# Hybrid decoder trunk, one core: the conditioning sum of the expert stage in its first blocks, the second mixer's sums in its attention, and another pace of the gathers

## The chip, the cores and the metric

The kernel runs on one core of one Trainium2 chip. The metric is the time of one execution on the device, in microseconds (us), as the median of several runs. The numbers of the profile come from one profiled execution of the same program. MB and GB are powers of ten.

## What is computed

A trunk of two residual layers over 512 positions of width 1024. Each layer is a token mixer and then a feed-forward part that retrieves experts by product keys. Before both, the input is normalized and modulated by shift, scale and gate vectors that come from a condition `c`:

```python
c_act = jax.nn.silu(c)
for layer in range(DEPTH):
    mod = (c_act @ ada_w[layer] + ada_b[layer])[:, None, :]
    sh1, sc1, g1, sh2, sc2, g2 = jnp.split(mod, 6, axis=-1)
    h = rmsnorm(x, norm_mix[layer]) * (1.0 + sc1) + sh1
    y = even_mixer(h, ...) if layer % 2 == 0 else odd_mixer(h, ...)
    x = x + g1 * y
    h = rmsnorm(x, norm_ffn[layer]) * (1.0 + sc2) + sh2
    x = x + g2 * peer_ffn(h, peer_w_q[layer], peer_sub_keys[layer], peer_u[layer], peer_v[layer])
return rmsnorm(x, norm_final)
```

`c_act @ ada_w` is a product of one row with a matrix of 1024 x 6144 per layer. The program calls each sixth of it (1024 x 1024, the pieces m = 0 to 5) a conditioning sum. Every position picks 128 experts (8 heads, 16 each) of 16384; an expert is one row of U and one of V:

```python
act = jax.nn.gelu(jnp.einsum('cd,ced->ce', xc, u[ec]))
return jnp.einsum('ce,ced->cd', gc.astype(xc.dtype) * act, v[ec])
```

## The kernel before, in words

**Whole program.** Four stages follow one another: the even mixer (layer 0), the expert stage of layer 0, the odd mixer (layer 1), the expert stage of layer 1. Each float32 product is made from three products of split operands (high and low part, `mm3`, lines 146 to 150): ScalarE makes the high part (line 162), VectorE the low part (line 163). The program is written as one sequence; a scheduler then sets the order on each engine, and each engine and each DMA queue works its list in that order. `issue_after` pins instructions behind a given one.

**The expert stage** (`peer`). Positions come in four blocks of 128. For the first three (384 positions) all 16384 experts are computed densely, in 128 blocks of 128 experts, and weighted by a gate matrix that is zero where an expert was not picked. For the last 128 positions the picked rows of U and V are gathered.

- Dense part: block i needs its U tile (512 KB; `u_block`, 24 matmuls of 384 columns, tile `ups`), then gelu (tile `gl`), the product with the gates (tile `wf`, line 1445), its split (`weh`, `wel`), its V tile (512 KB) and 18 matmuls of 512 columns that add to six PSUM banks `y`. Gate values come by DMA for eight blocks at a time (tile `gt`, 1.5 MB, line 1442). U and V tiles are loaded on the SP queue into tiles called `raw`, three buffers in all, which the whole program shares; the split tiles `wh`, `wl` have three buffers too. Already during routing 51 U blocks are computed ahead, so the main loop makes a U block and a V product in blocks 0 to 76 and a V product alone in blocks 77 to 124; three more V products follow at the end. These last 51 blocks are called the last stretch here.
- Gathered part (`gather_steps`): step k gathers 128 rows of U (tile `gu`, 128x1024, GpSimd's queue, line 1551), VectorE multiplies and sums them (line 1558); from step 16 on it also gathers the V rows of 16 steps before (`gv`), and VectorE adds them to the accumulator `acc` (128x1024 in SBUF, line 1566). From step 128 on only `gv` is left. How many steps are due at block i is set by two numbers: GU per block in blocks 0 to 76, GV per block after. `acc` is set to zero at the beginning of the stage (line 1427).
- Conditioning sum of the next layer (`ada_late`, first stage only): for each half of 512 columns, four loads of 512 KB (two pieces of the weights, tile `araw`, also in a `raw` buffer, line 259), two VectorE operations per load (lines 263 and 265) that add in a PSUM bank, a copy by ScalarE into another `raw` buffer (`asum`, line 268), and four small matmuls that sum over the partitions (line 271). It is put in from block 76 on, a quarter of a step per block (EP = 0.25).

**The odd mixer** (`odd`). Projections of V in two halves, then 64 attention units (8 head pairs, 2 heads, 4 position blocks) in a loop of 67 passes (`run_units`), with the remaining projections as filler. The four conditioning sums m = 2, 4, 3, 5 of layer 1 (`ada`, line 238 load of 256 KB in a `raw` buffer, lines 240 and 242 on VectorE) run as background, `self.bg`, 64 steps in all: `step(n % 2)` takes 12 of them in the second half of the V projection, and the attention loop takes OB = 0.75 per pass. What is left is done at the end.

## Time and profile before

| | |
|---|---|
| median of 3 runs | 3201.61 us (3197.92 to 3205.02) |
| profiled execution | 3189.73 us, span of its instructions 3187.9 us |
| mean granted TensorE clock | 0.992 |
| even mixer, layer 0 | about 0 to 350 us |
| expert stage, layer 0 | main loop from 746 us, last stretch 1394 to 1625 us |
| odd mixer, layer 1 | about 1625 to 1940 us |
| expert stage, layer 1 | main loop from 2321 us, last stretch 2969 to 3179 us |

PE is TensorE, PEld its weight loads, DVE VectorE, ACT ScalarE, POOL GpSimd, SP the engine whose queue issues most loads; a "q" behind the name means the queue. A window's row gives, for each engine, the busy time in us and the number of instructions, then the granted TensorE clock (1.00 is 2.4 GHz), the mean busy share of the 16 DMA engines and the rate. A wait's row gives who waited for whom, the sum, the number and the longest. A timeline's row ends with the idle time of the engine before it and what ended it.

### The profile page before, as it was taken

The numbers are of one execution on the slowest core, as the hardware profiler recorded it, in microseconds if no ns is written. First come the engines' busy times: TensorE is split into PE (matmuls) and PEld (weight loads), VectorE is DVE, ScalarE is ACT, GpSimd is POOL, SyncE is SP. The second block draws the span as 40 slices with busy tenths as digits, with TensorE's granted clock in tenths as the row PEclk, the third lists the DMA queues.
The fourth block names the chain that finished last, engine by engine and source line by source line (L and its number), as shares of the span: only waits on it lengthen the run. The fifth ranks groups of instructions, "written<-read, shape, count | busy, mean of one in ns | idle before, by whom it ended". The sixth has DMA issues, their size and how long they took to land.

```text
span 3187.9 us, 45266 instructions
## 1 busy us (share of the span) xinstructions
PE 3089.2 (97%) x16416; PEld 2681.4 (84%) x16416; DVE 2593.8 (81%) x5112; ACT 1371.3 (43%) x2294; POOL 711.3 (22%) x564
## 2 busy tenths in 40 slices
PE   8999999999999999998999999999999999999998
PEld 5766788998998898987777878899989998899887
DVE  6988799996777777887766888999867887788887
ACT  5566524553333333333355764245533333333333
POOL 0000000002444444432210000000024444444331
PEclk9999999999999999999999999999999999999999
DMA  7325323658899899997733333245588998899885
GB/s 244 133 86 175 108 90 124 229 223 290 290 319 331 320 336 325 334 320 282 264 129 129 127 109 112 93 171 224 216 289 317 324 338 325 314 328 336 310 318 191
DMA packets 304064, 758.91 MB, mean 238 GB/s; under 512 B 24328, under 2 KB 125248, under 8 KB 297696
## 3 DMA queue, kind: packets, MB, share of 16 engines
q1 hardware_dynamic: 225120, 480.04, 42.8%
q0 software_dynamic: 74240, 268.54, 23.2%
q10 hardware_dynamic: 4480, 7.44, 0.7%
q8 instruction: 128, 2.10, 0.3%
q14 instruction: 96, 0.79, 0.1%
HBM read 698.96 MB, written 56.64 MB: 237 GB/s over the span
## 4 chain that ended last, share of the span: by engine, by line
PE 60%; DMA 17%; DVE 16%; issue 4%; ACT 3%; POOL 0%; SPq 0%; DVEq 0%; ACTq 0%; POOLq 0%
DMA gv<-in_peer_v_dram,eidx 9%; PE ups L150 7%; PE y L149 7%; PE y L148 7%; PE y L150 7%; PE ups L148 7%; PE ups L149 7%; DVE wl L163 3%; PE pp L149 3%; PE pp L148 3%; PE pp L150 3%; DMA araw<-in_ada_w_dram 2%; DMA raw<-in_peer_v_dram 2%; DMA gu<-in_peer_u_dram,eidx 2%; PE gps L1312 1%
## 5 line engine op out<-in xcount | busy, mean ns | idle before, releaser
L162 ACT ACTIVATE wh<-raw 128x1024 fp32r<-128x1024 f32 x602 | 635.6, 1056 | 1015.6 <-PE ups L149 472.2
L163 DVE TENSOR_TENSOR wl<-raw,wh 128x1024 fp32r<-128x1024 f32 x602 | 734.2, 1220 | 111.3 <-ACT wh L162 110.2
L148 PE MATMUL ups<-h2h,wh 128*128 128x384 f32 x2048 | 693.0, 338 | 9.4 <-ACT h2h L162 4.8
L150 PE MATMUL ups<-h2h,wl 128*128 128x384 f32 x2048 | 693.7, 339 | 7.3 <-DVE wl L163 7.2
L149 PE MATMUL ups<-h2l,wh 128*128 128x384 f32 x2048 | 689.5, 337 | 0.7 <-DVE h2l L163 0.7
L1551 POOL DMA_INDIRECT gu<-in_peer_u_dram,eidx x256 | 290.4, 1134 | 1608.0 <-DVE eidx L1410 1165.1
L148 PE MATMUL y<-wh,weh 128*128 128x512 f32 x1536 | 602.3, 392 | 19.8 <-ACT wh L162 10.7
L149 PE MATMUL y<-wl,weh 128*128 128x512 f32 x1536 | 603.9, 393 | 3.1 <-DVE wl L163 3.1
L150 PE MATMUL y<-wh,wel 128*128 128x512 f32 x1536 | 602.7, 393 | 0.0
L1551 POOL DMA_INDIRECT gv<-in_peer_v_dram,eidx x256 | 395.9, 1546 | 555.2 <-DVE gu L1558 360.6
L1566 DVE SCALAR_TENSOR_TENSOR acc<-gv,act,acc 128x1024 f32<-128x1024 f32 x256 | 328.3, 1282 | 152.4 <-DMA gv<-in_peer_v_dram,eidx 151.5
L148 PEld LDWEIGHTS ups<-h2h,wh 128*128 128x128 f32 x2048 | 385.7, 188 | 17.9 <-ACT h2h L162 5.3
L150 PEld LDWEIGHTS ups<-h2h,wl 128*128 128x128 f32 x2048 | 385.2, 188 | 12.5 <-DVE wl L163 12.4
L149 PEld LDWEIGHTS ups<-h2l,wh 128*128 128x128 f32 x2048 | 385.6, 188 | 7.7 <-DVE h2l L163 1.2
L1558 DVE SCALAR_TENSOR_TENSOR gu<-gu,htm 128x1024 f32<-128x1024 f32 x256 | 312.3, 1220 | 60.5 <-DMA gu<-in_peer_u_dram,eidx 60.2
L148 PEld LDWEIGHTS y<-wh,weh 128*128 128x128 f32 x1536 | 290.1, 189 | 79.7 <-ACT wh L162 12.4
L149 PEld LDWEIGHTS y<-wl,weh 128*128 128x128 f32 x1536 | 289.9, 189 | 63.9 <-DVE wl L163 6.3
L150 PEld LDWEIGHTS y<-wh,wel 128*128 128x128 f32 x1536 | 289.7, 189 | 60.9 <-DVE wel L163 0.2
L162 ACT ACTIVATE weh<-wf 128x384 fp32r<-128x384 f32 x256 | 133.5, 524 | 480.8 <-PE y L149 356.0
L163 DVE TENSOR_TENSOR wel<-wf,weh 128x384 fp32r<-128x384 f32 x256 | 141.6, 554 | 81.3 <-ACT weh L162 80.5
L1445 DVE TENSOR_TENSOR wf<-gl,gt 128x384 f32<-128x384 f32 x256 | 140.0, 553 | 11.5 <-DMA gt<-gates 10.7
L1189 ACT ACTIVATE gl<-ups 128x384 f32<-128x384 f32 x256 | 121.4, 474 | 0.1
(411 smaller groups left out, 4252.2 us busy)
## 6 DMA issues: line engine op xcount, KB each, us to landing
raw<-in_peer_uT_dram SPq DMA_DIRECT2D x256, 512.0 KB, 4.5
raw<-in_peer_v_dram SPq DMA_DIRECT2D x256, 512.0 KB, 4.3
gates<-gst SPq DMA_DIRECT2D x48, 1024.0 KB, 5.0
gt<-gates SPq DMA_DIRECT2D x32, 1536.0 KB, 12.4
araw<-in_ada_w_dram SPq DMA_DIRECT2D x176, 256.0 KB, 3.1
raw<-in_peer_wq_dram SPq DMA_DIRECT2D x32, 512.0 KB, 3.3
raw<-in_odd_w_dram SPq DMA_DIRECT2D x25, 512.0 KB, 3.3
raw<-in_even_w_dram SPq DMA_DIRECT2D x23, 512.0 KB, 3.4
```

The lines of the kernel that those rows point to most:

```text
L148: mm(out, a[0], b[0], start=start, stop=False)
L149: mm(out, a[0], b[1], start=False, stop=False)
L150: mm(out, a[1], b[0], start=False, stop=stop)
L162: self.lact = nc.scalar.activation(hi, src, AF.Copy)
L163: self.last = nc.vector.tensor_tensor(lo, src, hi.bitcast(F32), op=ALU.subtract)
L1189: nc.scalar.activation(gl, ps[:, :ND], AF.Gelu_apprx_tanh)
L1312: nc.tensor.matmul(ps[:, z], oh[:, t, 1], og[:, t, 0], start=True, stop=False)
L1445: nc.vector.tensor_tensor(wf.rearrange("p (c t) -> p c t", t=CT), gls[i].rearrange("p (c t) -> p c t", t=CT), self.gt[:, :, i % IG], op=AL ...
L1551: nc.gpsimd.indirect_dma_start(out=r, out_offset=None, in_=table, in_offset=bass.IndirectOffsetOnAxis(ap=eidx[:, k:k + 1], axis=0))
L1558: nc.vector.scalar_tensor_tensor(r, r, 1.0, htm, op0=ALU.mult, op1=ALU.mult, accum_out=act[:, k:k + 1])
L1566: nc.vector.scalar_tensor_tensor(acc, r, act[:, j:j + 1], acc, op0=ALU.mult, op1=ALU.add)
```

## The change

Four things are done.

1. The conditioning sum of the first expert stage (`ada_in` in place of `ada_late`) is put in from block 0 on, one step per block, and adds in the two halves of `acc` in SBUF. The copy by ScalarE and its `raw` buffer are gone; the small matmuls read `acc`.
2. `acc` is set to zero just ahead of gather step 16, the first that adds to it, in both expert stages.
3. GU goes from 1.44 to 1.40, GV from 0.62 to 0.70, in both expert stages.
4. In the odd mixer the sums start behind the V projection, and the attention loop takes one step per pass.

```diff
-GU = 1.44
-GV = 0.62
+GU = 1.4
+GV = 0.7
+GRP = 16
-EP = 0.25
-OB = 0.75
+OB = 1
...
-    def ada_late(self, layer, m, psum, tag):
+    def ada_in(self, layer, m, sums, psum, tag):
...
-            acc = self.bank(psum, tag)
+            acc = sums[:, s]
...
                 yield 1
-            sb = self.stream.tile([P, D], F32, tag="raw", name=self.nm("asum"))[:, :T]
-            nc.scalar.activation(sb, acc, AF.Copy)
             ps = self.bank(psum, tag)
             for b in range(4):
-                nc.tensor.matmul(ps[:, b:b + 1], sb[:, b * P:(b + 1) * P], self.ones[:, 0:1], start=True, stop=True)
+                nc.tensor.matmul(ps[:, b:b + 1], acc[:, b * P:(b + 1) * P], self.ones[:, 0:1], start=True, stop=True)
...
-            self.bg = [self.ada(layer, m, ah, psum, "tr", 0) for m in (2, 4, 3, 5)]
-            for n, _ in enumerate(more):
-                self.step(n % 2)
+            for _ in more:
+                pass
...
             fl.add("out", self.out_early(layer, I["odd_wo"], 0, psum, lambda: done))
+            self.bg = [self.ada(layer, m, ah, psum, "tr", 0) for m in (2, 4, 3, 5)]
...
         acc = fin.tile([P, D], F32, name=self.nm("acc"))
-        nc.vector.memset(acc, 0.0)
...
-        self.bg = [self.ada_late(l, m, self.pu, "u") for l, m in ([] if last else [(layer + 1, 0)])]
-        steps = 0.0
+
+        self.bg = [] if last else [self.ada_in(layer + 1, 0, acc, self.pu, "u")]
...
                 while ng < due:
+                    if ng == GRP:
+                        self.step(1000)
+                        nc.vector.memset(acc, 0.0)
                     ng += 1
                     next(gather, None)
-                if i >= NK - AHEAD:
-                    steps += EP
-                    self.step(int(steps))
-                    steps -= int(steps)
+                self.step(1)
```

How the order of the instructions moves is shown at three places. A row is line, operation, output, inputs and shape; the number behind a name tells the buffers apart.

SP at the start of the first expert stage, before (`gates` is the gate matrix on its way to memory, `in_peer_uT` and `in_peer_v` are U and V):

```order
L170 DMA raw_7999<-in_peer_v_dram 128x1024
L1317 DMA gates_3612<-gst_7714 128x2048
L170 DMA raw_8035<-in_peer_uT_dram 128x1024
L170 DMA raw_8068<-in_peer_v_dram 128x1024
L1442 DMA gt_7997<-gates_3612 128x24x128
L170 DMA raw_8101<-in_peer_uT_dram 128x1024
L1442 DMA gt_8539<-gates_3612 128x24x128
L170 DMA raw_8134<-in_peer_v_dram 128x1024
L170 DMA raw_8170<-in_peer_uT_dram 128x1024
L170 DMA raw_8203<-in_peer_v_dram 128x1024
```

and in the change:

```order
L170 DMA raw_7998<-in_peer_v_dram 128x1024
L1315 DMA gates_3612<-gst_7714 128x2048
L259 DMA araw_8034<-in_ada_w_dram 128x2x512
L1439 DMA gt_7996<-gates_3612 128x24x128
L170 DMA raw_8038<-in_peer_uT_dram 128x1024
L170 DMA raw_8071<-in_peer_v_dram 128x1024
L1439 DMA gt_8576<-gates_3612 128x24x128
L259 DMA araw_8104<-in_ada_w_dram 128x2x512
L170 DMA raw_8108<-in_peer_uT_dram 128x1024
L170 DMA raw_8141<-in_peer_v_dram 128x1024
```

The first gate tile stands ahead of the next U and V tile and behind the first load of the sum; from then on each U and V pair has a load of the sum ahead of it, eight in all.

VectorE at the same place, from the last step of routing, before:

```order
L1269 TENSOR_TENSOR r_7901<-m_1636_7895 128x128
L1427 MEMSET acc_7958 128x1024
L163 TENSOR_TENSOR wl_7906<-raw_7903,wh_7905 128x1024
L1410 TENSOR_TENSOR eidx_3322<-ef,r_7901 128x128
L163 TENSOR_TENSOR wl_8002<-raw_7999,wh_8001 128x1024
L163 TENSOR_TENSOR wl_8038<-raw_8035,wh_8037 128x1024
L1445 TENSOR_TENSOR wf_8005<-gl_3645,gt_7997 128x384
L1445 TENSOR_TENSOR wf_8074<-gl_3714,gt_7997 128x384
L163 TENSOR_TENSOR wel_8008<-wf_8005,weh_8007 128x384
```

and in the change:

```order
L1267 TENSOR_TENSOR r_7901<-m_1636_7895 128x128
L1408 TENSOR_TENSOR eidx_3322<-ef,r_7901 128x128
L163 TENSOR_TENSOR wl_7906<-raw_7903,wh_7905 128x1024
L163 TENSOR_TENSOR wl_8001<-raw_7998,wh_8000 128x1024
L1442 TENSOR_TENSOR wf_8004<-gl_3645,gt_7996 128x384
L1442 TENSOR_TENSOR wf_8077<-gl_3714,gt_7996 128x384
L163 TENSOR_TENSOR wel_8007<-wf_8004,weh_8006 128x384
L1555 SCALAR_TENSOR_TENSOR gu_8028,act<-gu_8028,htm_3321 128x1024
L1555 SCALAR_TENSOR_TENSOR gu_8031,act<-gu_8031,htm_3321 128x1024
L263 TENSOR_SCALAR acc_7958<-araw_8034,cact 128x512
L163 TENSOR_TENSOR wl_8041<-raw_8038,wh_8040 128x1024
L265 SCALAR_TENSOR_TENSOR acc_7958<-araw_8034,cact,acc_7958 128x512
```

The memset ahead of the index cast is gone and the cast stands first; the sum's operations come between the products of the gathers and the weight splits.

SP around the second gate tile of the last stretch of the first expert stage, before:

```order
L170 DMA raw_13787<-in_peer_v_dram 128x1024
L170 DMA raw_13823<-in_peer_v_dram 128x1024
L170 DMA raw_13853<-in_peer_v_dram 128x1024
L259 DMA araw_13889<-in_ada_w_dram 128x2x512
L1442 DMA gt_14182<-gates_3612 128x24x128
L170 DMA raw_13895<-in_peer_v_dram 128x1024
L170 DMA raw_13931<-in_peer_v_dram 128x1024
L170 DMA raw_13961<-in_peer_v_dram 128x1024
L170 DMA raw_13997<-in_peer_v_dram 128x1024
```

and around the first and second of them in the change:

```order
L1439 DMA gt_13912<-gates_3612 128x24x128
L170 DMA raw_13596<-in_peer_v_dram 128x1024
L170 DMA raw_13634<-in_peer_v_dram 128x1024
L170 DMA raw_13672<-in_peer_v_dram 128x1024
L170 DMA raw_13708<-in_peer_v_dram 128x1024
L170 DMA raw_13738<-in_peer_v_dram 128x1024
L170 DMA raw_13774<-in_peer_v_dram 128x1024
L170 DMA raw_13810<-in_peer_v_dram 128x1024
L170 DMA raw_13840<-in_peer_v_dram 128x1024
L170 DMA raw_13876<-in_peer_v_dram 128x1024
L170 DMA raw_13914<-in_peer_v_dram 128x1024
L1439 DMA gt_14184<-gates_3612 128x24x128
```

A load of the sum that stood after every four V tiles, once directly ahead of a gate tile, stands there no more.

## Rows read from the trace of the kernel before

**Rows 1.** The page's first part, the whole span.

```profile
PE 3089.2 (97%) x16416; PEld 2681.4 (84%) x16416; DVE 2593.8 (81%) x5112; ACT 1371.3 (43%) x2294; POOL 711.3 (22%) x564
```

**Rows 2.** Windows: length, busy by engine, clock, DMA share, GB/s; both last stretches.

```profile
1394.00:1625.50 231.50, 218.21 (x949) 177.55 (x948) 183.68 (x249) 88.67 (x125) 59.62 (x48) 0.98 0.77 268
2969.00:3179.50 210.50, 210.36 (x924) 172.72 (x922) 169.60 (x227) 80.52 (x116) 61.00 (x43) 1.00 0.76 273
```

**Rows 3.** Waits, last stretch of the first expert stage: total us, times, longest.

```profile
ACT wh L162 <- DMA raw<-in_peer_v_dram: 59.3, 19, 12.8
```

**Rows 4.** Timeline of SP, ScalarE and TensorE around the first stop there.

```profile
1425.63 0.38 SPq L1442 DMA_DIRECT2D gt<-gates  x1
1426.76 17.10 SPq L170 DMA_DIRECT2D raw<-in_peer_v_dram  x4
...
1441.19 1.06 ACT L162 ACTIVATE wh<-raw 128x1024 fp32r<-128x1024 f32 x1 [9.82 <-DMA raw<-in_peer_v_dram]
...
1442.30 0.50 PE L148 MATMUL y<-wh,weh 128*128 128x512 f32 x1 [3.16 <-ACT wh L162]
```

**Rows 5.** Windows: the stage's start, the first stop, a shorter stop.

```profile
746.00:757.00 11.00, 10.77 (x44) 9.42 (x45) 9.69 (x17) 4.12 (x8) 4.02 (x4) 0.79 0.96 327
...
1439.00:1449.30 10.30, 6.38 (x20) 4.82 (x20) 6.86 (x9) 4.24 (x6) 1.68 (x1) 0.83 0.62 227
...
1523.60:1532.00 8.40, 5.62 (x24) 4.43 (x24) 6.37 (x8) 4.53 (x6) 1.68 (x1) 1.00 0.73 263
```

**Rows 6.** Windows: blocks 1 to 76 of both expert stages, and the first nine of these.

```profile
757.00:1394.00 637.00, 633.43 (x3192) 573.82 (x3191) 499.67 (x631) 223.30 (x311) 276.83 (x208) 1.00 0.90 321
2331.00:2969.00 638.00, 633.43 (x3193) 574.01 (x3192) 499.94 (x631) 223.64 (x311) 276.99 (x208) 1.00 0.90 321
757.00:830.00 73.00, 73.00 (x370) 66.35 (x369) 49.17 (x69) 26.21 (x37) 23.50 (x17) 1.00 0.74 262
```

**Rows 7.** The odd mixer: windows of V projection and attention; waits of TensorE.

```profile
1659.00:1692.00 33.00, 26.52 (x112) 19.33 (x112) 17.39 (x25) 11.76 (x16) 2.23 (x4) 0.96 0.56 179
1700.00:1900.00 200.00, 192.34 (x1029) 160.69 (x1028) 161.17 (x377) 141.25 (x326) 6.45 (x12) 0.98 0.32 109
...
PE pp L148 <- ACT wh L162: 1.4, 2, 0.9
PE pp L149 <- DVE wl L163: 0.4, 1, 0.4
...
PE pp L149 <- DVE ptl L526: 2.7, 1, 2.7
```

**Rows 8.** Windows: rates in the last stretches, second stage and first stage.

```profile
2969.00:3087.00 118.00, 118.00 (x523) 97.72 (x522) 97.72 (x133) 43.47 (x59) 45.57 (x33) 1.00 0.87 312
...
1400.00:1500.00 100.00, 90.36 (x384) 73.39 (x383) 77.67 (x108) 30.47 (x41) 31.59 (x24) 0.95 0.82 285
```

**Rows 9.** Timeline, second stage behind a gate tile: low part made, then read.

```profile
3049.09 1.22 DVE L163 TENSOR_TENSOR wl<-raw,wh 128x1024 fp32r<-128x1024 f32 x1
...
3050.89 0.39 PE L149 MATMUL y<-wl,weh 128*128 128x512 f32 x1
```

**Rows 10.** Timeline of VectorE and SP at the start of the first expert stage.

```profile
729.30 0.91 DVE L1427 MEMSET acc<- 128x1024 f32 x1 [0.16 <-issue]
...
745.07 1.03 DVE L1445 TENSOR_TENSOR wf<-gl,gt 128x384 f32<-128x384 f32 x2 [5.53 <-DMA gt<-gates]
...
731.83 0.38 SPq L1442 DMA_DIRECT2D gt<-gates  x1
```

**Rows 11.** Sum operations: into SBUF, into PSUM; ns min/median/max, first and last start.

```profile
L242 DVE SCALAR_TENSOR_TENSOR adacc<-araw,cact,adacc x126: 729/746/754, 51.5 to 1906.4; 128x512 f32<-128x512 f32 x126
...
L265 DVE SCALAR_TENSOR_TENSOR u<-araw,cact,u x14: 747/750/756, 1397.0 to 1532.3; 128x512 f32<-128x512 f32 x14
```

**Rows 12.** The gathers on GpSimd: ns min/median/max, first and last start.

```profile
L1551 POOL DMA_INDIRECT gu<-in_peer_u_dram,eidx x256: 936/1010/1989, 732.5 to 3055.0; - x128
L1551 POOL DMA_INDIRECT gv<-in_peer_v_dram,eidx x256: 933/1678/2614, 807.2 to 3138.9; - x128
```

More of the change, by code (lines that the diff above doesn't have):

```diff
@@ L1546, in gather_steps @@
         nc, I = self.nc, self.I
-        grp = 16
+        grp = GRP
         def fetch(table, k, tag):
```

## The prediction, made before the result

> **What bounds the kernel now.** I read the page first, then the busy table of single stretches, the waits inside them, and last the timeline at the stops. TensorE is busy 97% of the span [rows 1], so only three things can make the kernel shorter: TensorE time without work, TensorE time at the lower clock, or less work. The change takes no matmul of weight away, so I looked for the stretches in which TensorE is not full. The two expert stages hold the same work, and only the first one carries a conditioning sum. That makes the second a yardstick. Its last 51 blocks (77 to 127, after the up-projection has run out) take 210 us with TensorE busy 210.4 of them; in the first stage the same 51 blocks take 230 us, with 13.3 us of idle TensorE and a mean granted clock of 0.98 [rows 2]. ScalarE, which makes the high part of each V weight tile, waits 59 us in that stretch for the tile's DMA [rows 3]. One of the stops shows how this reaches TensorE: the gate tile (1.5 MB) is issued at 1425.6 and the V loads from 1426.8 behind it; the V tile lands at 1441.2, and TensorE has then stood for 3.2 us [rows 4]. A stop costs more than its idle time: around this one, and at the start of the stage, the granted clock is 0.83 and 0.79, so for a part of the window it was 1.2 GHz and not 2.4; after a shorter stop (2.8 us idle of 8.4) it stayed 1.00 [rows 5].
>
> Elsewhere the expert stage is close to full: blocks 1 to 76 lose 3.6 us of TensorE in the first stage and 4.6 us in the second [rows 6]. The second mixer has 6.5 us idle in the end of its V projection and 7.7 us in 200 us of attention [rows 7].
>
> **The change part by part.**
>
> (a) *The eight 512 KB loads of the sum leave the last 51 blocks.* With them go the ScalarE copy and the tile that it held. The bound is the yardstick: the stretch falls from 231.5 to 210.5 us on the same cuts, 21 us, of which I take 20, because the end of the first stage also feeds the next layer. **-20 us** (not more than -21).
>
> (b) *GV goes from 0.62 to 0.70.* Each step gathers two tiles of 128x1024 f32 (0.524 MB), so a block of the last stretch moves 0.524 (V) + 0.197 (an eighth of a gate tile) + 1.4 x 0.524 = 1.455 MB where it moved 1.371. A block lasts 210.4 / 51 = 4.125 us: 352 GB/s are asked for where 332 were. This lasts until 128 steps are reached: 77 x 1.40 = 107.8 at block 77, then 20.2 / 0.70 = 29 blocks. It applies to both stages. In the second stage 312 GB/s were moved in the 118 us in which 332 were asked for [rows 8]; the difference came out of the lead of the loads. At its worst place the V tile landed so late that its low part was ready at 3050.3, and TensorE read it at 3050.9 [rows 9]: 0.6 us were left. The additional 29 x 0.084 = 2.4 MB take 7.8 us at 312 GB/s. The first part of them eats lead that is still there. Lower end 0 (TensorE did not stop at 332 asked for); upper end 7.8 plus 2 for clock, 10 per stage. I take 5 per stage, nearer to the row with 0.6 us left: **+10 us**. The Trainium skill (DMA: Bandwidth & Descriptors, section Where 436 GB/s comes from) gives about 358 GB/s as the HBM side's limit for one core; by it 352 would still pass, (b) would be 0 and the sum 10 us lower. The trace shows 312 with a growing lag, so the measurement decides, and I keep the +10.
>
> (c) *GU goes from 1.44 to 1.40.* 77 x 0.04 = 3.1 steps, 3.2 MB less in blocks 0 to 76 of each stage, 10 us of transfer at the 321 GB/s of that stretch [rows 6]. Only lost TensorE time can come back: 3.6 and 4.6 us. I take 3.5 each: **-7 us** (0 to -9, with clock).
>
> (d) *The memset of the accumulator leaves the start of the stage.* It takes 0.9 us on VectorE just ahead of a weight split and of the cast of the expert indices; the gate tile follows on SP at 731.8, and its landing ends a 5.5 us wait of VectorE, while TensorE has nothing to do [rows 10]. In the new order the gate tile stands one place earlier and the memset is gone. In the first stage the sum's first load is now ahead of it (512 KB). I take -2 in the second stage and -1 in the first: **-3 us** (0 to -7, if the stop gets so short that the clock stays up). The memset itself now comes at block 11 on VectorE, which is busy 49 of 73 us in this part [rows 6]: 0, and 0.9 us per stage without that cover.
>
> (e) *The sum in blocks 0 to 8.* SP now issues sum, U, V in each block, through the same three buffers. VectorE gets 16 operations of 0.75 us (into SBUF as into PSUM the same [rows 11]), 12 us over 75 us, where it has 24 us free; the DMA share there is 0.74 [rows 6], because up to block 11 the gathers fetch only U rows. So neither runs full: the cost is the lead of the loads, which falls by a third, since three tiles per block share three buffers. Queued behind a late sum load are the next U and V loads on SP, and on VectorE the weight splits that TensorE waits for. Lower end 0; upper end the price of (a), 20. I take **+2.5 us**. The 16 small matmuls of the sum move from a stretch with idle TensorE to one without: about 0.2 us each in part hidden before, **+1 us**.
>
> (f) *The second mixer.* Twelve of 64 steps leave the V projection; its weight loads no longer share buffers with them, and 1.8 us of waits for weights there can go [rows 7]. They go into the attention, at 1.0 instead of 0.75 steps per pass: 67 passes held 50 steps and now hold all 64, 14 x 0.75 = 10.5 us more of VectorE, which is busy 161 of 200 us there [rows 7]. The rest that stood at the mixer's end is gone: TensorE waits 2.7 us there for a low part that VectorE makes behind operations of the sums [rows 7], of which I take 1. Covered, the extra costs 2 us; without cover 10.5. Net **-1 us** (-3 to +8).
>
> Sum: -20 + 10 - 7 - 3 + 2.5 + 1 - 1 = **-17.5 us**. The profiled execution took 3189.7 us, so it would take 3172.2. The median of the runs, 3201.6, lies 11.9 above that execution; against the median the forecast is **3184 us**.
>
> **The rivals.**
>
> *The gathers starve both last stretches* (slower). If the queues move no more than the 285 GB/s of 1400 to 1500 us [rows 8], the 29 blocks need 42.2 MB / 285 = 148 us where TensorE needs 119.6 and a lead of three tiles (1.57 MB at 312 GB/s) covers 5: 23 us per stage, 46 in place of 10. Sum +18.5: 3220 us. It decides once (b) costs more than 27.5 in all, so below 42.2 / (119.6 + 5 + 13.75) = 305 GB/s. For it: 312 is not far, and the lag was growing. Against it: the 285 comes from a stretch that stopped, where nothing was asked for during part of the time, and blocks 1 to 76 move 321 [rows 6].
>
> *The stops move along with the loads* (no change). Each load of the sum cost 20 / 8 = 2.5 us where it stood; if it costs that in blocks 0 to 8 as well, (e) is 20: sum 0, 3201.6 us. For it: the same three buffers, three loads per block and not one in four. Against it: 74% DMA share and twice the time per block.
>
> *VectorE shuts GpSimd out* (a smaller gain). The trace shows index gathers of 1.01 us in the median beside the U products and 1.68 beside the accumulation [rows 12], 0.67 us apart. The accumulation of the sum now has two inputs in SBUF; 14 x 0.67 = 9.4 us of GpSimd in blocks 0 to 8. If all of it reached TensorE: 3193.5. The Trainium skill (SBUF — State Buffer, section SBUF: two separate sides) says that a VectorE operation with two SBUF inputs holds the port pair that a GpSimd operation reading SBUF needs; the two durations agree. But GpSimd is busy 23.5 of 73 us there [rows 6].
>
> *The attention pays in full*: (f) is +8, 3193 us. It needs VectorE in the chain of nearly every pass; TensorE's 7.7 us idle in 200 speak against it.
>
> **How the numbers follow.** Forecast 0.68, starved stretches 0.10, stops moved 0.11, port 0.04, attention 0.07. The measurement tells 0.2% (6.4 us) from no change, so faster means below 3195.2. The forecast falls there in 19 of 20 cases, port and attention mostly, moved stops in about one of four: faster 0.77, same 0.13, slower 0.10. The low end takes (b) at 0 and (d) full: 3201.6 - 33 = 3168. The high end reaches to the moved stops: 3202. Above it lie mainly the starved stretches.
>
> **What would show it.** Right: the last 51 blocks of the first stage near 215 us at clock 1.00, no ScalarE wait for V above 6 us there; V tiles in the last stretch of the second stage late behind the gate tiles, and a few stops of 1 to 3 us that were not there before; less idle TensorE in blocks 1 to 76; the first gate tile 1 to 2 us earlier after the index cast. Wrong: a last stretch of the second stage above 225 us (starved), idle TensorE above 8 us in blocks 0 to 9 (stops moved), or an attention longer by more than 5 us.

## The result and the profile after

The kernel after took **3166.35 us** (median of 4 runs, 3162.26 to 3175.49) beside 3203.32 us for the kernel before (4 runs, 3197.92 to 3210.42): ratio **0.9895, 95% interval 0.9865 to 0.9924**, or 24 to 43 us faster. A second comparison gave 3169.38 beside 3195.83 us, ratio 0.9927, 0.9901 to 0.9954. By their ratios the two comparisons say 34 and 23 us. The sign of the prediction held. Of its range, 3168 to 3202 us, the first comparison meets the low end (0.9895 of the 3201.6 that the forecast starts from is 3168; the 3166.35 itself lies 1.7 below) and the second lies inside (3178). The 17.5 us of its sum did not hold. So terms were mis-sized.

The profiled execution of after took 3165.39 us, span 3163.6, mean granted clock 0.996. Within one comparison, single executions of before lie up to 29 us apart and those of after up to 15, so the traces are compared by pieces, two executions of each kernel. One of the ten executions of run 2 took 6707.7 us, twice the others, and is in no ratio. A piece runs between the first matmuls of two places in TensorE's timeline ("search" is the first matmul of the first U block that a stage computes ahead, tile `ups`; the query products of its product-key search, tile `qps`, begin 11 to 14 us later; block 0, 1, 9, 77 and 127 are the first matmuls of these V products). Times in us:

| piece | before, two traces | after, two traces | change of the means | in the prediction's sum |
|---|---|---|---|---|
| up to the first search | 363.0, 366.9 | 363.4, 364.4 | -1.0 | 0 |
| first stage, search to block 1 | 393.8, 394.3 | 387.0, 385.1 | -8.0 | -1 (d) |
| blocks 1 to 9 | 66.5, 66.5 | 77.5, 76.3 | +10.4 | +3.5 (e) |
| blocks 9 to 77 | 570.9, 570.2 | 570.4, 567.4 | -1.7 | -3.5 (c) |
| blocks 77 to 127 | 226.5, 223.9 | 210.9, 214.5 | -12.5 | -15 (a, b) |
| block 127 to the second search | 317.4, 319.6 | 308.6, 309.1 | -9.7 | -1 (f) |
| second stage, search to block 1 | 392.9, 393.8 | 386.7, 387.7 | -6.2 | -2 (d) |
| blocks 1 to 9 | 66.5, 66.5 | 66.5, 66.5 | 0 | 0 |
| blocks 9 to 77 | 571.7, 571.9 | 569.2, 567.2 | -3.6 | -3.5 (c) |
| blocks 77 to 127 | 206.1, 206.1 | 210.7, 212.3 | +5.4 | +5 (b) |

The changes add to -26.9; the means of the two spans differ by 26.8. The windows of after that answer to [rows 2, 6, 7] (length, busy by engine, clock, DMA share, GB/s): blocks 1 to 9, blocks 9 to 77 and the last stretch of the first stage, the last stretch of the second, the V projection.

```profile
750.40:827.90 77.50, 72.45 (x354) 64.66 (x353) 55.91 (x84) 25.58 (x36) 17.17 (x14) 0.96 0.85 292
827.90:1398.30 570.40, 566.76 (x2858) 513.82 (x2857) 448.71 (x560) 199.89 (x277) 250.06 (x189) 1.00 0.92 323
1398.30:1609.30 211.00, 208.53 (x915) 170.24 (x914) 174.80 (x232) 83.64 (x117) 67.99 (x53) 1.00 0.81 288
2940.10:3150.80 210.70, 207.54 (x905) 169.23 (x905) 172.76 (x230) 78.98 (x112) 67.37 (x49) 1.00 0.82 288
1647.70:1680.70 33.00, 31.59 (x137) 24.36 (x136) 14.21 (x18) 14.54 (x19) 2.23 (x4) 1.00 0.41 136
```

The last stretch of the first stage now reads like that of the second: 2.5 and 3.2 us without work, clock 1.00. ScalarE's wait for V tiles there, against [rows 3], in the waits of after:

```profile
ACT wh L162 <- DMA raw<-in_peer_v_dram: 27.3, 11, 6.4
```

So 59 became 27 us and the longest 12.8 became 6.4. That was the reason I gave for the change, and it is there. The sign that I had named, no such wait above 6 us, was just missed. But half of the net gain in the pieces (14.2 of 26.9 us) came from the two starts, which I had costed at 3 us together, and a third (9.7) from the second mixer, costed at 1; the sum in its new place took 10.4 back where I had 3.5.

**The starts.** VectorE, SP and TensorE at the start of the second stage, first of before, then of after (start, duration, engine, instruction, idle before it and its releaser):

```profile
2304.34 0.91 DVE L1427 MEMSET acc<- 128x1024 f32 x1 [0.16 <-issue]
2305.17 1.16 DVE L163 TENSOR_TENSOR wl<-raw,wh 128x1024 fp32r<-128x1024 f32 x1
2306.25 0.28 DVE L1410 TENSOR_TENSOR eidx<-ef,r 128x128 int32<-128x128 f32 x1
...
2306.36 0.33 SPq L170 DMA_DIRECT2D raw<-in_peer_v_dram  x1
2306.98 0.38 SPq L1442 DMA_DIRECT2D gt<-gates  x1
...
2319.79 1.03 DVE L1445 TENSOR_TENSOR wf<-gl,gt 128x384 f32<-128x384 f32 x2 [5.22 <-DMA gt<-gates]
...
2320.96 0.79 PE L148 MATMUL y<-wh,weh 128*128 128x512 f32 x1 [4.41 <-ACT weh L162]
```

```profile
2283.99 0.29 DVE L1408 TENSOR_TENSOR eidx<-ef,r 128x128 int32<-128x128 f32 x1
...
2284.42 0.38 SPq L1439 DMA_DIRECT2D gt<-gates  x1
...
2286.06 2.06 SPq L170 DMA_DIRECT2D raw<-in_peer_v_dram  x1
...
2291.71 1.03 DVE L1442 TENSOR_TENSOR wf<-gl,gt 128x384 f32<-128x384 f32 x2 [1.51 <-DMA gt<-gates]
```

Without the memset the index cast no longer stands behind a weight split, the gate tile is issued right after it and ahead of a V load, and its landing lets VectorE go on 7.3 us after the issue, where it took 12.8 (the last section has the spread of this over all traces). TensorE had stood 4.41 us there (4.72 in the first stage) and then took 9.9 and 10.5 us for the first block instead of 8.3; in after it does not stand, and the blocks take 8.3 and 8.5.

**The V projection.** VectorE and TensorE at the place where the second mixer changes PSUM pools, before and after:

```profile
1683.21 0.75 DVE L242 SCALAR_TENSOR_TENSOR adacc<-araw,cact,adacc 128x512 f32<-128x512 f32 x1 [0.86 <-DMA araw<-in_ada_w_dram]
1686.79 0.75 DVE L242 SCALAR_TENSOR_TENSOR adacc<-araw,cact,adacc 128x512 f32<-128x512 f32 x1 [2.83 <-DMA araw<-in_ada_w_dram]
1687.46 1.88 DVE L163 TENSOR_TENSOR vcl<-pp,vch 128x512 fp32r<-128x512 f32 x3
...
1690.39 0.68 DVE L163 TENSOR_TENSOR vcl<-pp,vch 128x512 fp32r<-128x512 f32 x1
...
1691.12 0.80 PE L148 MATMUL pp<-hTh,wh 128*128 128x512 f32 x1 [4.55 <-DVE vcl L163]
```

```profile
1670.06 2.67 DVE L163 TENSOR_TENSOR vcl<-pp,vch 128x512 fp32r<-128x512 f32 x4 [1.77 <-ACT vch L162]
...
1672.79 0.50 PE L148 MATMUL pp<-hTh,wh 128*128 128x512 f32 x1 [1.41 <-DVE vcl L163]
```

In before a step of the sum stands ahead of V's low parts in VectorE's queue and waits 2.83 us for its own load. TensorE then stops for 4.55 us, and behind the stop the granted clock is lower. The windows behind it, in before and then in after, read 0.74 and 1.00:

```profile
1692.00:1700.00 8.00, 8.00 (x28) 6.37 (x28) 2.94 (x5) 1.39 (x3) 0.00 (x0) 0.74 0.54 185
```

```profile
1680.70:1690.00 9.30, 9.21 (x43) 7.00 (x41) 7.88 (x13) 3.20 (x5) 0.00 (x0) 1.00 0.54 169
```

### The profile page after: what moved, and what is told of

Read it like the earlier page. It is cut to its first block, busy times and chain, and to the rows that moved or that the text cites. A ratio compares the mean times of both kernels' runs of the same rounds, so it can differ in the third digit from the quotient of the medians.

```text
span 3163.6 us, 45286 instructions
## 1 busy us (share of the span) xinstructions
PE 3080.8 (97%) x16416; PEld 2675.2 (85%) x16416; DVE 2590.2 (82%) x5112; ACT 1371.6 (43%) x2292; POOL 710.2 (22%) x564
## 4 chain that ended last, share of the span: by engine, by line
PE 55%; DMA 19%; DVE 16%; issue 6%; ACT 3%; POOL 1%; DVEq 0%; ACTq 0%; SPq 0%; POOLq 0%
DMA gv<-in_peer_v_dram,eidx 11%; PE ups L150 7%; PE ups L148 7%; PE ups L149 7%; PE y L149 7%; PE y L150 7%; PE y L148 7%; DVE wl L163 3%; PE pp L148 2%; PE pp L149 2%; PE pp L150 2%; DMA gu<-in_peer_u_dram,eidx 2%; DMA araw<-in_ada_w_dram 2%; PE gps L1310 1%; DMA raw<-in_odd_w_dram 1%
```

## The experiments

Ratios are against the kernel before, run beside each.

**1. The kernel before again.** No edit.

> The kernel before, unchanged. Theory (the profiled execution of before was a short one of its kind, 3189.7 against a median of 3203.3): the executions here have a median of 3200 to 3206, and their granted clock is lower in the longer ones; the new profiled execution lies at 3195 to 3207 and is longer in the last 51 blocks of the first expert stage (more or longer stops than 12.5 us of idle TensorE) or at lower clock, nowhere else. Rival (the profile costs nothing and timing runs have something of their own): the new profile gives 3189 +- 2 with the same stops, and the timed runs 3203.

3195.71 us (10 runs, 3184.5 to 3202.0), ratio 0.9995 (0.9973 to 1.0017); its profiled execution took 3194.2. The pieces stand in the table: the new trace is not longer in the last stretch (223.9) than the first (226.5). So the place I expected the difference at was wrong, and so was the median of 3200 to 3206. The 3189.7 us that my sum started from is a low value within the spread; against the later medians of before, 3193 to 3198, the anchor was not far off, and the first median of 3203 was a high one.

**2. The memset alone.** Before, with one line moved:

```diff
-        nc.vector.memset(acc, 0.0)
...
                 while ng < due:
+                    if ng == 16:
+                        nc.vector.memset(acc, 0.0)
```

> The kernel before with one line moved: the accumulator is cleared just ahead of gather step 16 and not at the start of the stage. Theory (the memset holds up the index cast by 2 us, the gate tile falls behind a V load and the gathers start with it, and its landing then stops TensorE): in both stages the stop before the first product of y (4.72 and 4.41 us) is gone or under 1 us, the first two blocks are 6 us earlier each, 12 us in all, so -10 to -14 us against before. Rival (what I forecast, the memset and its place in line only): -2 us in each stage, a stop of 2 to 3 us left and the clock still low in the first block: -4. Other rival (the start changed through the sum and the gather rate, not the memset): the stops stay at 4 to 5 us, 0.

Ratio 0.9971 (0.9948 to 0.9993). Both stops are gone. The first block of each stage, which was [rows 5] at clock 0.79 in before:

```profile
745.80:754.20 8.40, 8.40 (x45) 7.66 (x44) 7.39 (x12) 3.45 (x5) 3.98 (x3) 1.00 1.09 381
2322.80:2331.10 8.30, 8.30 (x44) 7.56 (x43) 7.18 (x12) 3.44 (x5) 4.09 (x3) 1.00 1.09 380
```

Search to block 1 takes 387.7 and 386.9 us (393.8 and 392.9): these 12 to 13 us are the memset's, as the theory said. But the whole was only 9 us faster (2 to 17): in this trace blocks 9 to 77 took 573.6 and 577.1 us. I had not expected that, and it led to runs 8 and 11.

**3. The memset on GpSimd, at its old place.**

```diff
-        nc.vector.memset(acc, 0.0)
+        nc.gpsimd.memset(acc, 0.0)
```

> The kernel before with the memset at its old place but on GpSimd instead of VectorE. Theory (what cost 6.5 us per start is the index cast's place in VectorE's queue: 2 us later there puts the gate tile behind one more V load, and its landing stops TensorE): as with the memset moved away, the first product of y comes 4 to 5 us earlier in both stages and the next block 2 us earlier, 8.3 to 8.5 us for the first block where it took 10.5. Rival (the gathers, which GpSimd issues and which now wait for the memset there, set the start): first product of y as in before, 383 us after the search's start, or later. Total -5 to -10 against before, since blocks 9 to 77 gave back 3 to 5 us per stage when the memset alone was moved.

Ratio 0.9951 (0.9932 to 0.9970). Search to block 1: 387.7 and 386.7 us. VectorE and SP at the start of the first stage, where [rows 10] had the memset:

```profile
731.60 0.29 DVE L1410 TENSOR_TENSOR eidx<-ef,r 128x128 int32<-128x128 f32 x1
...
731.95 0.38 SPq L1442 DMA_DIRECT2D gt<-gates  x1
...
733.66 2.54 SPq L170 DMA_DIRECT2D raw<-in_peer_v_dram  x1
...
742.41 1.03 DVE L1445 TENSOR_TENSOR wf<-gl,gt 128x384 f32<-128x384 f32 x2 [4.62 <-DMA gt<-gates]
```

The memset is still done at the start, and the gain is the same. So it is the index cast's place in VectorE's queue that counted, and with it the gate tile's place on SP. One changed word makes the kernel 10 to 22 us faster than before; its ratio stays above both of after's.

**4. The second mixer's part alone.**

```diff
-            self.bg = [self.ada(layer, m, ah, psum, "tr", 0) for m in (2, 4, 3, 5)]
-            for n, _ in enumerate(more):
-                self.step(n % 2)
+            for _ in more:
+                pass
...
+            self.bg = [self.ada(layer, m, ah, psum, "tr", 0) for m in (2, 4, 3, 5)]
...
-OB = 0.75
+OB = 1
```

> The kernel before with the second mixer's part alone: none of its sums' 64 steps in the V projection, one step per pass in the attention. Theory (the sums' steps in the V projection held VectorE and the loads, and made the 4.55 us stop before the low part of V and the low clock after it): the V projection with that stop is 8 to 10 us shorter (78.7 us from the last product of the first expert stage to the first score), attention and tail within 2 us, sum -7 to -10 us. Rival (my forecast): V projection -2, attention +2, end -1: -1 us. The expert stages are untouched: their block times should read as in before.

Ratio 0.9974 (0.9950 to 0.9998), 1 to 16 us faster. Block 127 to the first score: 75.0 us, where six traces with the old mixer have 82.0 to 85.6; the attention 203.9 and the rest 33.0, as in before. The stop before V's low part in its waits:

```profile
PE pp L148 <- DVE vcl L163: 1.4, 1, 1.4
```

In the pieces block 127 to the second search takes 311.9 us where before has 317.4 and 319.6: 5.5 to 7.7 us less, at the lower edge of the theory. The expert stages were expected to read as in before, and the first did not: its blocks 9 to 77 took 577.8 us (570.2 and 570.9 in before) and its last stretch 229.6 (223.9 and 226.5), with nothing changed there. So a long piece of a single trace can be off by 7 us; runs 8, 9 and 11 are to be read with that in mind.

**5. The sum alone (with its memset).** After, with the old mixer (the lines of run 4 turned round) and

```diff
-GU = 1.4
-GV = 0.7
+GU = 1.44
+GV = 0.62
```

> The kernel after with the old gather rates (1.44 and 0.62) and the old second mixer: only the sum is moved, and the memset with it. Theory: last 51 blocks of the first stage (77 to 127) as in the second stage of before, 206 us from block 77 to 127 (226.5 before): -20; both starts -6 each: -12; the sum in blocks 0 to 8 costs 10 to 13 us there. Sum -19 to -22. Rival (the sum costs nothing at its new place and the 10 us that blocks 1 to 76 lost in after come from the rate 1.40): blocks 1 to 76 of the first stage as in before (637 us), sum -32.

Ratio 0.9935 (0.9915 to 0.9955), 14 to 27 us. The last stretch of the first stage:

```profile
1401.40:1608.50 207.10, 207.06 (x914) 170.43 (x914) 167.81 (x222) 83.62 (x116) 63.77 (x46) 1.00 0.80 278
```

Without the new rate it runs almost without a stop (0.04 us without work), 17 to 19 us shorter than in before. Blocks 1 to 9 take 73.5 us, 7 more; the theory had 10 to 13 for the sum there.

**6. The kernel after again.** No edit.

> The kernel after, unchanged, beside the kernel before on this chip. Expected 3162 to 3172 us, 0.988 to 0.992 of before, and the same segments as in its first profile: block 1 to 9 of the first stage 75 to 78 us, 127-to-first-score 75 us.

3169.38 us, ratio 0.9927, a little above the range of ratios that I expected; the pieces are in the table.

**7. After without the sum.**

```diff
-        self.bg = [] if last else [self.ada_in(layer + 1, 0, acc, self.pu, "u")]
+        self.bg = []
+        if not last:
+            self.done.add((layer + 1, 0))
+            nc.vector.tensor_copy(self.mod[:, layer + 1, 0], self.adab[:, layer + 1, 0])
```

> The kernel after without the sum in the first expert stage (left out: the weighted sum of the next layer's first modulation column; only its bias is written). Theory (the sum in the first blocks is paid there, through stops of TensorE behind its loads and the low clock after them): block 1 to 9 of the first stage falls from 77.5 to 66.5 us as in the second stage, nothing else moves, -8 to -11 us against after. Rival (the stops there come from the two gate tiles and the gathers, and the sum only rides along; my forecast of 3.5): block 1 to 9 stays above 72 us, 0 to -4.

3158.44 us, ratio 0.9887 (0.9866 to 0.9909), 10.9 us below after beside it. Blocks 1 to 9:

```profile
751.40:817.90 66.50, 66.50 (x338) 60.45 (x337) 45.48 (x64) 24.25 (x34) 17.68 (x13) 1.00 0.78 274
```

At these rates the 10 to 11 us that these blocks lost go with the sum alone. With the old rates the same sum costs 6 to 7 there (73.5 us in run 5 and 72.8 in run 11, against 76.3 to 77.5 in three traces with both the sum and 1.40); no run shows why. In after 5.05 of them are idle TensorE (77.5 - 72.45), about 3 the clock (0.04 x 77.5); the rest isn't resolved. The larger stops are two. TensorE at the first, and then SP, ScalarE and TensorE at the second, all of after:

```profile
756.70 0.44 PE L148 MATMUL ups<-h2h,wh 128*128 128x384 f32 x1 [1.94 <-ACT wh L162]
...
771.26 0.38 SPq L259 DMA_DIRECT2D araw<-in_ada_w_dram  x1
774.48 0.33 SPq L170 DMA_DIRECT2D raw<-in_peer_uT_dram  x1
...
778.57 0.38 SPq L1439 DMA_DIRECT2D gt<-gates  x1
779.23 5.11 SPq L170 DMA_DIRECT2D raw<-in_peer_v_dram  x1
...
790.25 1.06 ACT L162 ACTIVATE wh<-raw 128x1024 fp32r<-128x1024 f32 x1 [7.22 <-DMA raw<-in_peer_v_dram]
...
791.36 0.51 PE L148 MATMUL y<-wh,weh 128*128 128x512 f32 x1 [1.70 <-ACT wh L162]
```

The second is the stop of [rows 4] on a smaller scale: a V load behind a gate tile, with a third tile in the same three buffers.

**8. The memset and the new rates, on before.** Run 2 and

```diff
-GU = 1.44
-GV = 0.62
+GU = 1.4
+GV = 0.7
```

> The kernel before with the memset just ahead of gather step 16 and the rates 1.40 and 0.70; sum and second mixer as before. With the memset alone the starts gained 13 us in the profile but blocks 9 to 77 took 573.6 and 577.1 us where they had taken 571 and 572, and the median gained 8. Theory (blocks 9 to 77 are bound by the transfers at 1.44, so an earlier start is given back there; 1.40 takes 68 x 0.04 gathers pairs or 2.9 MB out of them): blocks 9 to 77 at 569 to 571 us in both stages, the second stage's blocks 77 to 127 at 210 to 211 (206.1), the first stage's at 228 to 236; together -8 to -13 us against before. Rival (the give-back was chance, and the rates only move gathers from one stretch to the other): blocks 9 to 77 at 574 to 577, total -3 to -8.

Ratio 0.9984 (0.9961 to 1.0007), which can't be told from before. By that ratio it gained 5 us (-2 to 12), inside the rival's 3 to 8 and below the theory's 8 to 13. Blocks 9 to 77 took 567.9 us in the first stage, below the theory's 569 to 571, but 573.4 in the second. The last stretch took 233.3 us in the first stage, as the theory said, and 207.6 in the second, where it said 210 to 211. Inconclusive by itself.

**9. The sum from block 2 on.**

```diff
-                self.step(1)
+                if i >= 2:
+                    self.step(1)
```

> The kernel after with the sum's first step at block 2 and not at block 0. Theory (the first stop, at 754.8, comes from two sum loads that meet the two gate tiles of the start): that stop and its low clock go, block 1 to 9 takes 71 to 74 us, -3 to -6 us against after. Rival (the 4.2 MB cost their transfer time wherever they stand in these blocks, 4.2 MB at 320 GB/s = 13 us less what slack there is): the stops move to blocks 3 to 10, the same time within 2 us.

3168.28 us beside 3169.38: the same. Blocks 1 to 9 took 74.5 and blocks 9 to 77 572.6, together 647.1, where after has 647.9 and 643.7. The stop at 754.8 is gone, but one of 2.31 us came at 796.2. This agrees with the rival (the cost moves with the loads); with pieces and medians that vary by several us it does not exclude the theory's 3.

**10. The sum in the first mixer.**

```diff
-MA = [(0, 4), (0, 3), (0, 5)]
-EA = (2.4, 1.7)
+MA = [(0, 4), (0, 3), (0, 5), (1, 0)]
+EA = (2.7, 2.3)
...
-        self.bg = [] if last else [self.ada_in(layer + 1, 0, acc, self.pu, "u")]
+        self.bg = []
```

> The kernel after with the sum of the first expert stage made in the first mixer instead: its 16 steps (16 loads of 256 KB, 16 operations of 0.75 us on VectorE) join the 48 that run beside the attention there, which steps 2.7 and 2.3 per pass instead of 2.4 and 1.7; the expert stage carries no sum. Theory (the sum costs 10.5 us in the first blocks because it stands beside gate tiles, gathers and two weight loads per block; in the first mixer, from 210 to 363 us, TensorE is idle for 13 us and VectorE busy 78%, so about 12 us more of VectorE are half covered): block 1 to 9 of the stage 66.5 us, -10; the start of the first stage's product-key search (363 to 368 us now) 3 to 7 us later; sum -3 to -8 us against after, 3161 to 3166 where after has 3169. Rival (VectorE sets the pace of the first mixer's attention): that start 12 us later or more, 0 to +3 against after.

3171.6 us (6 runs, 3159.1 to 3179.7), ratio 0.9914 (0.9888 to 0.9940): no better than after. Blocks 1 to 9 fell to 66.5, but the first search began at 375.9, 12 us later than in after (8 to 13 later than in the other traces, 363.0 to 367.7). That is the rival's number. Its reason is not shown: VectorE is busy 78 and 77% of the two windows from 210 us to the first search, as in after (79 and 77%). What differs most is the granted clock, 0.91 and 0.95 where after has 0.98 and 1.00:

```profile
210.00:310.00 100.00, 91.41 (x394) 63.91 (x393) 78.19 (x168) 58.41 (x135) 0.00 (x0) 0.91 0.58 190
310.00:376.00 66.00, 58.50 (x269) 44.39 (x267) 50.57 (x96) 38.12 (x88) 0.00 (x0) 0.95 0.39 131
```

That is 0.07 x 100 + 0.05 x 66 = 10 us, an estimate from these rows. TensorE's longest wait for a sum there is not for the moved one, which comes last, but for one of the three that stood there before and now run at the higher pace. In after the longest of this kind is 2.86 us; here it is 4.74:

```profile
284.65 1.84 PE L246 MATMUL tr<-ones,adacc 128*128 128x1 f32 x8 [4.74 <-DVE adacc L242]
```

**11. Both old rates in after.** After, with the four lines on the rates of run 5.

> The kernel after with both old rates, 1.44 and 0.62; the moved sum, the moved memset and the new second mixer stay. Theory (the rates only move the gathers: what 1.40 gives in blocks 9 to 77 comes back as stops in blocks 77 to 127, 4 to 6 us per stage each way): blocks 9 to 77 at 572 to 576 us in both stages (567 to 570 with the new rates), blocks 77 to 127 at 206 to 208 (211 to 214), the total within 4 us of after. Rival (my forecast, +10 for the second rate and -7 for the first): 3 us below after, which this measurement can't tell from 0; other rival (the second rate costs nothing and the first saves 10): 8 to 10 us above after.

3167.07 us (6 runs), ratio 0.9916 (0.9894 to 0.9938): as after. Blocks 9 to 77 and the last stretch of each stage:

```profile
823.70:1397.80 574.10, 568.40 (x2859) 513.54 (x2858) 456.67 (x570) 200.16 (x278) 259.18 (x195) 1.00 0.92 326
1397.80:1604.80 207.00, 206.96 (x913) 170.38 (x912) 167.99 (x222) 83.35 (x116) 62.38 (x46) 1.00 0.80 280
2367.80:2943.70 575.90, 569.51 (x2858) 515.01 (x2857) 456.93 (x572) 200.53 (x278) 256.38 (x195) 1.00 0.92 324
2943.70:3150.50 206.80, 206.35 (x905) 169.35 (x905) 165.52 (x220) 78.43 (x111) 60.97 (x42) 1.00 0.80 281
```

What the new rates give in blocks 9 to 77 (4 to 9 us per stage) they take in the last stretch (4 to 7.5) and in blocks 1 to 9 of the first stage (3.5 to 4.7). The rates are worth nothing that can be measured.

**12. The second rate alone undone.** After with

```diff
-GV = 0.7
+GV = 0.62
```

> The kernel after with the second rate alone undone (0.62 in place of 0.70; the first stays 1.40). Theory (0.70 costs 4 to 6 us in each last stretch, as forecast): blocks 77 to 127 take 206 to 208 us in both stages up to the accumulator's end, but at block 120 about 10 gather steps are left instead of 6, which costs 2 to 5 us there; together -2 to -8 us against after. Rival (the last stretch is at its limit either way and the leftover steps of block 120 decide): 77 to 127 stays at 210 to 214, 0 to +5.

3163.06 us (4 runs), ratio 0.9905 (0.9873 to 0.9936): not told from after. In blocks 77 to 118 each block takes its 4.1 us in both stages: no stop at all. At block 120 the steps that are left come all at once, and block 122 takes 8.8 and 9.9 us; TensorE there, first and second stage:

```profile
1584.84 0.79 PE L149 MATMUL y<-wl,weh 128*128 128x512 f32 x1 [2.70 <-DVE wl L163]
```

```profile
3125.26 0.80 PE L149 MATMUL y<-wl,weh 128*128 128x512 f32 x1 [2.65 <-DVE wl L163]
```

Blocks 77 to 127 take 212.2 us in both stages, as in after: the loss has moved to another block. No experiment gave a version that is measurably faster than after and computes the whole.

## Why the prediction was right in kind and short by a third

**(a) The loads leave the last stretch: right.** -20 was forecast; with the sum alone moved it is -17 to -19 in the pieces, and the yardstick of the second stage was the right bound.

**(b) GV: right.** +5 per stage was forecast; the second stage's last stretch shows +4.6 and +6.2. In run 8, without the moved sum, it was +1.5. The mechanism is the one forecast, lead that is used up first and then stops, but the 312 GB/s of [rows 8] was no limit: the first 82 us pass without a stop at 333 GB/s, then the stops come at 288:

```profile
2940.10:3022.00 81.90, 81.90 (x363) 67.81 (x363) 69.25 (x95) 30.04 (x41) 34.21 (x27) 1.00 0.92 333
3022.00:3055.00 33.00, 29.84 (x127) 23.23 (x126) 26.80 (x37) 9.48 (x14) 12.71 (x10) 1.00 0.86 288
```

By the 358 GB/s of the Trainium skill (DMA: Bandwidth & Descriptors, section Where 436 GB/s comes from) the term would have been 0; the trace does not reach it in this stretch, while the first blocks of run 2 moved 380 GB/s over 8 us. So the stretch's own rows decide.

**(c) GU: right in size against the same start.** -3.5 per stage was forecast. Against the old rates with the new start (run 11) it is 4 to 9; against before it is 1.7 and 3.6, which would fit an earlier start that, at the old rate, costs part of itself there (see (d)). (b) and (c) together were +3 in the sum; run 11 shows no difference.

**(d) The memset: the largest error.** The step that failed is "I take -2 in the second stage and -1 in the first", with "0 to -7" for both. Measured at its place: -8.0 and -6.2. I priced the 2 us by which the index cast comes earlier, and one place on SP. The shorter flight of the gate tile was not in it (7.3 us instead of 12.8 in the second stage), although the order shown ahead of the prediction has it pass a V load. The bound was wrong too: each stage has a stop of 4.4 to 4.7 us and then some 2 us of low clock (as in [rows 5]), so it is 13 and not 7. How much of the 13 us lasts to the end is less sure. Runs 2 and 3 were 9 and 16 us faster (2 to 17, 10 to 22). In the traces of these two, with the old rates, the second stage from search to block 127 took 1236.5 and 1238.9 us, within 2 us of before (1237.1 and 1238.3); with the new start and GU at 1.40 it took 1232.5 to 1234.2 in seven traces. Run 11, with the new start and the old rates, had 1237.0. That fits a stage that its transfers bound, in which an earlier start is lead lost later; but run 5, with the old rates too, had 1233.6, the profiled executions of runs 2 and 3 were 7 and 8 us above the medians of their kernels, and the new rates on the old start were not tried alone. So this stays open.

**(e) The sum in the first blocks: too cheap.** The step "I take **+2.5 us**" (and 1 for the small matmuls) measured 10.4, shown by run 7 for these rates. My reason, 74% DMA share and VectorE time to spare, was an average over 73 us; in after the larger stops come at the two places where a gate tile stands beside the sum's load. The bounds, 0 to 20, held it in the middle, and I took a value near the lower end without a row for it.

**(f) The second mixer: the second error.** "1.8 us of waits for weights there can go" took the small part of [rows 7]. Of the 6.5 us of idle TensorE in that window, which the prediction names, it costed no more than these; 4.55 of them are one stop, put at nothing without a reason. VectorE's rows show it behind a step of the sum that waits for its load, and the lower clock after it comes on top. -1 was forecast, -9.7 measured in the pieces, and run 4 shows the V projection's part alone (75.0 us against 82.0 to 85.6). It does not separate the held-up VectorE from the buffers that the sum's loads no longer take. The attention took the 14 steps for nothing: 201.5 and 201.1 us where it had 202.7 and 204.1.

So against the pieces the sum of -17.5 was short by 11.2 in (d), 8.7 in (f) and 1.0 before the first search, where the change does nothing, and too good by 6.9 in (e), 2.9 in the last stretches and 1.7 in (c): together the 9.4 us that are missing. The low end of the range was added up wrongly too: (b) at 0 and (d) full take 14 from the sum, which makes -31.5 and 3170 us, not -33 and 3168.

Of the rivals, the starved stretches did not come (210.7 us, not above 225). The stops did move with the loads, at half their price: 10.4 us against 20. VectorE did not shut GpSimd out: the gathers of blocks 0 to 8 take 1.67 us in the median with the sum and 1.68 without it, so the rule of the Trainium skill on two SBUF inputs (SBUF — State Buffer, section SBUF: two separate sides) costs nothing that shows here. The premise was misread as well: [rows 12] groups the gathers by table, not by what VectorE does beside them, and in blocks 0 to 8 of before the 15 gathers of U already take 1.68 us in the median. The attention paid nothing. Of the signs, idle TensorE in blocks 1 to 76 fell in the second stage (4.6 to 3.1 us) and rose in the first (3.6 to 8.7), by the sum.

## What to carry to other kernels

Where an engine works a queue in order, look for the operation that stands just ahead of the last link before a stop: a 0.9 us memset or a background step that waits for its own load can hold up a whole engine, and the price is the stop, the slower clock after it, and the flight of whatever is issued late. Cost a stop by the whole of what it can give back, in every stage in which it occurs. A background piece of 4 MB cost 6 to 11 us in the first blocks, depending on the pace of the gathers, about 12 in the first mixer and 17 to 19 in the last stretch: find the cheapest place, and do not expect a free one. A piece of one trace moves by several us from one execution to the next, so a term of 3 us needs more than one trace.

## What was unexpected of the hardware

The first gate tile of a stage (1.5 MB) needed 12.3 to 13.2 us from issue to use in the six starts with the old order, behind a V load (before, its repeat and run 4). In the 22 starts with the new order it needed 6.8 to 7.6 us in 14 and 9.0 to 11.9 in eight. So the order on the queue is not all that sets the flight, and no run shows what else does. One 512 KB load at the 320 GB/s of the stage would be 1.6; the gathers that start beside it may be part of the rest, which no run separated. TensorE's stop was 3.9 to 4.7 us in the six and 0 to 1.1 in the 22, those with a long flight too: the issue, about 2 us earlier (the memset's 0.91 and the weight split's 1.16 ahead of the cast), counts beside the flight.

A stop's length alone did not tell what the clock did after it. It was 0.79 in the block after a stop of 4.7 us [rows 5] and 0.74 in the 8 us after one of 4.55; it stayed 1.00 where 2.8 of 8.4 us were idle [rows 5]; and in the window of after around two stops of 1.94 and 0.65 us, the first from 754.8 on, it was 0.88. Two nearly equal pairs of stops differ most. In before, 2.02 and 0.76 us are the idle time of that window of [rows 5] with 1.00; in after, a window of the same length with 1.70 and 0.76 us has 0.80. No run shows what makes the difference.

```profile
751.00:765.00 14.00, 11.41 (x48) 9.83 (x47) 9.94 (x15) 3.43 (x5) 3.62 (x3) 0.88 0.90 323
789.40:797.80 8.40, 5.95 (x20) 4.39 (x19) 6.43 (x9) 3.96 (x5) 1.68 (x1) 0.80 0.61 200
```

The pair of stops of before:

```profile
1525.65 0.50 PE L148 MATMUL y<-wh,weh 128*128 128x512 f32 x1 [2.02 <-ACT wh L162]
1526.91 0.50 PE L149 MATMUL y<-wl,weh 128*128 128x512 f32 x1 [0.76 <-DVE wl L163]
```
